# Latent attention scores as five fp32r products per pair of heads, each head on 64 rows

## The chip, the cores and the metric

The kernel runs on one core of one Trainium2 chip. A core has one TensorE (PE in the profile, its weight loads PEld), VectorE (DVE), ScalarE (ACT) and GpSimd (POOL), each working through its own instructions in the order in which the program lists them, and 16 DMA engines that are fed from queues, here those of SyncE (SP) and GpSimd. TensorE multiplies a stationary tile, loaded into the array beforehand, with a moving tile and adds into PSUM; the other engines read PSUM and SBUF. The metric is the device time of one execution in microseconds (us).

## The reference: what is computed

A decoder trunk of two layers over 512 tokens of width 1024, in float32. Layer 0 is a pooling and convolution mixer; layer 1 is multi-head latent attention, the part that changes. Each layer is followed by cross-attention into 256 memory tokens and a gated MLP.

```python
def mla_attention(h, cos, sin, ...):          # 16 heads, NOPE 64, ROPE 32, V_HEAD 64
    cq, ckv, k_pe = split(h @ w_dq_dkv, [384, 640])
    q = (rmsnorm(cq) @ w_uq).reshape(b, t, 16, 64 + 32)
    q_nope, q_pe = q[..., :64], apply_rope(q[..., 64:])
    kv = (rmsnorm(ckv) @ w_ukv).reshape(b, t, 16, 64 + 64)
    k_nope, v = kv[..., :64], kv[..., 64:]
    k_pe = apply_rope(k_pe)                   # one rotary key for all heads
    # per block i of 128 queries:
    s = (q_nope . k_nope + q_pe . k_pe) / sqrt(96)
    s = where(kpos <= qpos, s, -1e30)
    o = softmax(s) @ v
    return o @ w_o
```

Every score is thus a sum over 96 products: 64 of the content part, which has its own key per head, and 32 of the rotary part, whose key the heads share.

## The kernel before, in words

**Arithmetic.** Most products are made from fp32r operands. A float32 matrix is split into a high part (the value cast to fp32r) and a low part (the rest), and one product is three matmuls into the same PSUM bank: high by high, high by low, low by high (`mm3`, L177-181). A matrix is split in one of three ways: `load_w` (L168-175) fetches a weight by an SP DMA into `wr`, ACT casts it into `wh` (L173) and DVE subtracts into `wl` (L174), with both put early in the order (high priority); `low_by_dma` (L164-167) has ACT write minus the raw weight into `wl` and a GpSimd DMA add the raw weight to `wl`; `split_psum` (L207ff) has ACT cast a PSUM bank (L211) and DVE subtract (L212). The MLP's weights use the second way, with two buffers each of `wh1` and `wl1`.

**The stage.** `latent_attention` makes the low-rank queries `cq` (three 128-row tiles, high and low) and keys `ckv` (two tiles), then the one rotary key. After that come four groups of four heads. `group(g)` makes the four heads' rotary queries (`lin`, 9 matmuls of 512 columns) and turns them (`rotate`: a shuffle and three multiplications or sums on DVE); from the weights `ukv` and `uqn` it makes the content keys and queries (`contents`: `nope`, two banks of keys with 6 matmuls each, two of queries with 9 each). Two heads share a bank of 128 rows, 64 each. `group_values(g)` makes the values (`v`, 24 matmuls of 256 columns, two DVE copies).

**Scores before.** Each head has one operand of 128 rows for the query and one for the key: 64 rows of content, 32 of rotary part, 32 of zeros (kind A leaves the zeros off and uses 96). Four layouts, `qA`..`qD` and `kA`..`kD`, serve the four heads of a group. ACT copies the rotary rows (four copies of 32 rows, L1217, for a query) and one content half of each bank (64 rows, L1231), DVE the other half (L1232). `scores(n)` then makes four native float32 matmuls, one for each block of 128 queries against 128, 256, 384 and 512 keys (L1273, `s`; blocks 0 and 2 share a bank). DVE adds the mask and takes the row maximum of each block (L1275, called mask below), ACT makes the exponentials (L1281, four per head), DVE normalises (L1286).

**Around it.** `turn(n)` transposes the ten causal 128 by 128 blocks of a head's probabilities on PE (`t`, L1298) and ACT copies them out (L1300); `values(p)` multiplies those of two heads with `v` (L1310, `mpv`, two heads in the two halves of 64 columns). The loop over heads makes scores of head n, then, after every fourth head, the next group and its values, then `values` and `turn` of earlier heads (LAG = 2).

**What sets the order.** The program is written in this order and a scheduler places each engine's instructions by priority. At run time each engine keeps that order; an instruction that waits holds up all that stand behind it on its engine. PSUM has 8 banks, taken in turn.

Of the kernel before, what the change touches and what calls it, by code (L numbers as in the profile page):

```python
# [15 lines left out]
ALU = mybir.AluOpType  # L16
# [89 lines left out]
def kernel(ctx: ExitStack, tc: tile.TileContext, a):  # L106
# [988 lines left out]
    def rope_tables():  # L1095
# [41 lines left out]
    KIND = {  # L1137
        "A": (slice(0, 64), slice(64, 96), slice(96, 128)),
        "B": (slice(0, 64), slice(96, 128), slice(64, 96)),
        "C": (slice(64, 128), slice(0, 32), slice(32, 64)),  # L1140
        "D": (slice(64, 128), slice(32, 64), slice(0, 32)),
    }
    ORDER = ("A", "C", "B", "D")
    TILE = (("A", "C"), ("B", "D"))

    def latent_attention(norm, nxt, cs, sn, kv):
# [3 lines left out]
                           fill=NEG, base=0, channel_multiplier=1)  # L1150

# [17 lines left out]
        kacc, acc = slot("kacc"), slot("qacc")  # L1169
        kvp, cq, ckv = [], [], []  # L1170
# [29 lines left out]

        qb = {k: slot("q" + k) for k in KIND}
        kb = {k: slot("k" + k) for k in KIND}
        for k in KIND:
            for t in (qb[k], kb[k]):
                pool.memset(t[KIND[k][2], :], 0.0)

        def rotate(src, buf):
# [6 lines left out]
            vec.tensor_tensor(t, t, sw, ALU.add)  # L1214
            for k in KIND:
                rows = KIND[k][1]
                act.copy(buf[k][rows, :], t[rows, :])  # L1217
# [3 lines left out]
        rotate(kpe, kb)  # L1221

        def contents(buf, wh, wl, xs, nk):

            for i, (k0, k1) in enumerate(TILE):
# [4 lines left out]
                r0, r1 = KIND[k0][0], KIND[k1][0]  # L1230
                act.copy(buf[k0][r0, :], ps[r0, :])  # L1231
                vec.tensor_copy(buf[k1][r1, :], ps[r1, :])  # L1232
# [3 lines left out]
        kvw = {}  # L1236

        def group(g):

            rotate(linear(a["uqp"][g], cq), qb)  # L1240
            kvw[g] = wh, wl = load_w(a["ukv"][g], 1024)
            contents(kb, wh, wl, ckv, KKV)
            qh, ql = load_w(a["uqn"][g], 2 * KQ * P)
            contents(qb, qh, ql, cq, KQ)
# [18 lines left out]
        def scores(n):  # L1263
            kind = ORDER[n % 4]
            rows = slice(0, 96) if kind == "A" else slice(0, P)
            q, k = qb[kind][rows], kb[kind][rows]
            mx = small("mmx", [P, TB], bufs=3)
            banks = [bank("s") for _ in range(3)]
            ps = [banks[0][:, :P], banks[1][:, :2 * P], banks[0][:, P:], banks[2]]
            ts = [slot("p") for _ in range(3)]  # L1270
            ex = [ts[0][:, :P], ts[1][:, :2 * P], ts[0][:, P:], ts[2]]
            for i in (0, 2, 1, 3):
                pe.matmul(ps[i], q[:, i * P:(i + 1) * P], k[:, :P * (i + 1)], start=True, stop=True)  # L1273
            for i in (0, 2, 1, 3):
                vec.tensor_tensor_reduce(out=ex[i], in0=ps[i], in1=masks[:, T - P * (i + 1):], scale=1.0,  # L1275
                                         scalar=-3e38, op0=ALU.add, op1=ALU.max, accum_out=mx[:, i:i + 1])
# [36 lines left out]
        LAG = 2  # L1313
        proj = []
        group(0)
        for n in range(HEADS + LAG + 1):
            if n == HEADS:
                kv = fetch_kept(kv)
            if n < HEADS:
                scores(n)  # L1320
                if n == 0:
                    group_values(0)
                if n % 4 == 3 and n + 1 < HEADS:
                    group(n // 4 + 1)
# [126 lines left out]
```

## Time and profile before

| | |
|---|---|
| time, median of 3 runs | 1383.6 us (1383.36 to 1383.9) |
| the profiled execution | 1383.12 us, its span 1381.3 us |
| PE busy | 1352.6 us, 98% of the span |
| DVE busy | 1020.0 us, 74% |
| ACT busy | 748.8 us, 54% |
| the heads' part of latent attention, 738 to 868 us | 130 us |
| of it PE busy | 129.06 us |

The span is the time from the first to the last instruction that the profiler saw; the execution's own time is 1.8 us more. Busy time of PE counts matmuls whose ends are modelled, so a matmul of 512 columns shows 0.39 us though the next one starts 0.23 us later; spacings of starts are used below. In a timeline row the columns are the start and the length in us, the engine, the line, the operation, output and inputs, and how many instructions the row holds; a native float32 matmul shows as two instructions. Idle time before an instruction and what ended it stand in brackets.

### The profile page before, as it was taken

How to read it: one execution, taken by the hardware profiler on the slowest of the kernel's cores; microseconds unless marked ns; L12 is line 12 of the kernel's file. 1: busy time of each engine (PE TensorE's matmuls, PEld its weight loads, DVE VectorE, ACT ScalarE, POOL GpSimd, SP SyncE). 2: the span in 40 equal slices, each digit the busy share in tenths (PEclk: the TensorE clock that was granted, in tenths of full speed). 3: DMA queues.
4: the chain of work that ended last, by engine and by line, in shares of the span. 5: the costliest groups of instructions: out<-in, count | busy, mean ns of one | idle time of the engine just before them, and what ended most of it. 6: DMA issues, size and time to landing. Idle time of an engine off the chain costs nothing.

```text
span 1381.3 us, 20270 instructions
## 1 busy us (share of the span) xinstructions
PE 1352.6 (98%) x7756; PEld 1168.1 (85%) x7756; DVE 1020.0 (74%) x1897; ACT 748.8 (54%) x1264; POOL 52.9 (4%) x71
## 2 busy tenths in 40 slices
PE   8999999999989999999999999999999999999997
PEld 6888978888879999999887776888887899999987
DVE  6999989554787777776869775755549777777765
ACT  6416456445655555554447786644556555555433
POOL 0000000001100000000000000000011000000000
PEclk9999999999999999999999999999999999999999
DMA  9335634118835545553321113321486455555421
GB/s 327 99 104 188 217 104 151 61 38 207 184 91 130 159 124 138 134 137 94 106 81 50 43 47 107 107 77 61 124 188 124 130 132 143 134 136 144 111 73 62
DMA packets 57265, 168.01 MB, mean 122 GB/s; under 512 B 6480, under 2 KB 8144, under 8 KB 57168
## 3 DMA queue, kind: packets, MB, share of 16 engines
q1 hardware_dynamic: 47664, 135.55, 30.6%
q0 software_dynamic: 7776, 28.32, 12.3%
q10 hardware_dynamic: 1728, 2.86, 0.6%
q8 instruction: 60, 0.98, 0.3%
q14 instruction: 37, 0.30, 0.1%
HBM read 162.50 MB, written 4.19 MB: 121 GB/s over the span
## 4 chain that ended last, share of the span: by engine, by line
PE 88%; DVE 8%; ACT 2%; issue 1%; DMA 0%; SPq 0%; DVEq 0%; ACTq 0%
PE lin L179 11%; PE lin L181 11%; PE lin L180 11%; PE xyz L179 8%; PE xyz L180 8%; PE xyz L181 8%; PE down L180 4%; PE down L179 4%; PE down L181 4%; DVE cv L934 3%; PE s L1273 1%; PE mpv L1310 1%; DVE wl L174 1%; PE t L1298 1%; PE vx L180 1%
## 5 line engine op out<-in xcount | busy, mean ns | idle before, releaser
L179 PE MATMUL xyz<-th,wh 128*128 128x256 f32 x816 | 230.8, 284 | 10.6 <-ACT q L737 10.6
L181 PE MATMUL xyz<-th,wl 128*128 128x256 f32 x816 | 231.5, 284 | 0.0
L180 PE MATMUL xyz<-tl,wh 128*128 128x256 f32 x816 | 231.3, 284 | 0.0
L173 ACT CAST wh<-wr 128x1024 fp32r<-128x1024 f32 (+3 forms) x120 | 112.7, 944 | 161.8 <-issue 60.6
L179 PE MATMUL lin<-hh,wh 128*128 128x512 f32 x432 | 171.0, 396 | 5.9 <-ACT hh L286 5.9
L179 PEld LDWEIGHTS xyz<-th,wh 128*128 128x128 f32 x816 | 155.7, 192 | 23.2 <-ACT q L737 14.9
L180 PE MATMUL lin<-hl,wh 128*128 128x512 f32 x432 | 169.7, 393 | 0.0
L181 PE MATMUL lin<-hh,wl 128*128 128x512 f32 x432 | 169.2, 392 | 0.2 <-DVE wl L174 0.2
L180 PEld LDWEIGHTS xyz<-tl,wh 128*128 128x128 f32 x816 | 156.8, 192 | 7.1
L174 DVE TENSOR_TENSOR wl<-wr,wh 128x1024 fp32r<-128x1024 f32 (+3 forms) x120 | 130.1, 1086 | 42.4 <-ACT wh L173 40.9
L181 PEld LDWEIGHTS xyz<-th,wl 128*128 128x128 f32 x816 | 156.7, 192 | 0.0
L565 DVE TENSOR_TENSOR wl<-ws,wh 128x1024 fp32r<-128x1024 f32 x68 | 83.3, 1225 | 61.4 <-ACT wh L564 47.9
L564 ACT CAST wh<-ws 128x1024 fp32r<-128x1024 f32 x68 | 71.3, 1049 | 103.9 <-PE xyz L180 101.3
L179 PE MATMUL down<-fh,dwh 128*128 128x512 f32 x256 | 101.9, 398 | 1.2 <-ACT dwh L218 1.2
L180 PE MATMUL down<-fl,dwh 128*128 128x512 f32 x256 | 102.0, 398 | 0.0
L181 PE MATMUL down<-fh,dwl 128*128 128x512 f32 x256 | 100.5, 393 | 0.5 <-DVE dwl L219 0.5
L179 PEld LDWEIGHTS lin<-hh,wh 128*128 128x128 f32 x432 | 81.6, 189 | 22.3 <-ACT hh L286 6.2
L180 PEld LDWEIGHTS lin<-hl,wh 128*128 128x128 f32 x432 | 81.5, 189 | 18.5 <-DVE hl L287 2.7
L181 PEld LDWEIGHTS lin<-hh,wl 128*128 128x128 f32 x432 | 81.5, 189 | 17.5 <-DVE wl L174 0.6
L167 POOL DMA_DIRECT2D wl<-in_ffn_up x54 | 46.9, 868 | 1058.2 <-ACT wl L166 1058.2
L934 DVE SCALAR_TENSOR_TENSOR cv<-a,con,cv 128x509 f32<-128x509 f32 (+25 forms) x115 | 79.4, 726 | 0.1
L670 ACT ACTIVATE c<-c 128x512 f32<-128x512 f32 x44 | 27.8, 632 | 58.5 <-DVE c L669 58.3
(404 smaller groups left out, 3152.1 us busy)
## 6 DMA issues: line engine op xcount, KB each, us to landing
wr<-in_ffn_up SPq DMA_DIRECT2D x88, 512.0 KB, 4.1
wl<-in_ffn_up POOLq DMA_DIRECT2D x54, 512.0 KB, 5.7
dr<-in_ffn_down SPq DMA_DIRECT2D x64, 256.0 KB, 4.2
wr<-in_xa_wk SPq DMA_DIRECT2D x16, 512.0 KB, 3.5
wr<-in_xa_wv SPq DMA_DIRECT2D x16, 512.0 KB, 4.3
wr<-in_xa_wq SPq DMA_DIRECT2D x16, 512.0 KB, 3.5
wr<-in_xa_wo SPq DMA_DIRECT2D x16, 512.0 KB, 3.5
wr<-in_ffn_down SPq DMA_DIRECT2D x16, 384.0 KB, 3.3
```

The lines of the kernel that those rows point to most:

```text
L167: pool.dma_start(lo, src, accum_op=ALU.add)
L173: act.copy(hi[:, :n], raw[:, :n])
L174: vec.tensor_tensor(lo[:, :n], raw[:, :n], f(hi[:, :n]), ALU.subtract)
L179: pe.matmul(ps, ah, bh, start=first, stop=False, skip_group_check=more)
L180: pe.matmul(ps, ah, bl, start=False, stop=False, skip_group_check=more)
L181: pe.matmul(ps, al, bh, start=False, stop=last, skip_group_check=more)
L564: act.copy(hi[:, :n], raw)
L565: vec.tensor_tensor(lo[:, :n], raw, f(hi[:, :n]), ALU.subtract)
L670: act.activation(c, c, AF.Silu)
L934: vec.scalar_tensor_tensor(cv[i][:, s:], gl[i][:, :T - s], w, cv[i][:, s:], ALU.mult, ALU.add)
L1273: pe.matmul(ps[i], q[:, i * P:(i + 1) * P], k[:, :P * (i + 1)], start=True, stop=True)
L1298: pe.transpose(banks[b][:, c:c + P], prob[n][i][:, j * P:(j + 1) * P], ident)
```

## The change

1. Each pair of heads that shares a bank has its scores made together. The content queries and keys stay as high and low parts over 128 rows (`split_psum`, four per group in place of eight copies of 64 rows), head 0 in rows 0 to 63 and head 1 in rows 64 to 127. A block of scores is five fp32r matmuls for each head: high by high, high by low, low by high for the content, then two for the rotary part. The two heads' matmuls alternate and use rows 0 to 63 and 64 to 127 of the array.
2. For the rotary part, a head's 64 rows hold the query's high part in 32 rows and its low part in the other 32 (`rotary`: two ACT casts, four DVE subtractions of 32 rows). It is multiplied with `krh` (the key's high part in every 32 rows) and with `krl` (the key's low part under the query's high part, zeros elsewhere). The host puts the four heads' rotary columns in the order 0, 2, 1, 3.
3. The loop runs over pairs: blocks 0, 2, 1 of the pair, then `values` of the pair two back, `turn` of one earlier head, then block 3 and both softmaxes, then `turn` of the other head; after each second pair the next group with its values.
4. `ukv` and `uqn` no longer go through `load_w` but through `group_weights`: SP load, ACT cast into `wh1`, ACT negation into `wl1`, GpSimd DMA that adds. Group 0's weights are asked for at the start of the stage, group 1's after group 0's values, later ones two groups ahead.

The program has 256 matmuls more (scores 64 to 320), 8 DVE subtractions of weights fewer, 8 ACT negations and 8 GpSimd DMAs more.

```diff
+        def group_weights(g):
+            for src, n, out in ((a["ukv"][g], 1024, kvw), (a["uqn"][g], 2 * KQ * P, qw)):
+                raw = load_raw(src, n)
+                out[g] = hi, lo = early_parts()
+                act.copy(hi[:, :n], raw[:, :n])
+                low_by_dma(lo[:, :n], raw[:, :n], src)
...
         kacc, acc = slot("kacc"), slot("qacc")
+        group_weights(0)
...
-            for k in KIND:
-                rows = KIND[k][1]
-                act.copy(buf[k][rows, :], t[rows, :])
+            return t
...
-        rotate(kpe, kb)
+        t = rotate(kpe)
+        krh = slot("krh", F32R)
+        act.copy(krh, t)
+        krl = [slot("krl", F32R) for _ in range(2)]
+        for e in range(2):
+            pool.memset(f(krl[e]), 0.0)
+            for q in (e, e + 2):
+                r = slice(32 * q, 32 * q + 32)
+                vec.tensor_tensor(krl[e][r, :], t[r, :], f(krh[r, :]), ALU.subtract)
+
+        def rotary(src):
+            t = rotate(src)
+            out = []
+            for e in range(2):
+                q = slot("qr", F32R)
+                act.copy(q, t)
+                for h in range(2):
+                    r = slice(64 * h + 32 * e, 64 * h + 32 * e + 32)
+                    w = slice(64 * h + 32 * (1 - e), 64 * h + 32 * (1 - e) + 32)
+                    vec.tensor_tensor(q[w, :], t[r, :], f(q[r, :]), ALU.subtract)
+                out.append(q)
+            return out
...
-                r0, r1 = KIND[k0][0], KIND[k1][0]
-                act.copy(buf[k0][r0, :], ps[r0, :])
-                vec.tensor_copy(buf[k1][r1, :], ps[r1, :])
+                out.append(split_psum(ps, name))
+            return out
...
+            qr[g] = rotary(linear(a["uqp"][g], cq))
+            wh, wl = kvw[g]
+            kc[g] = contents(wh, wl, ckv, KKV, "kc")
+            qh, ql = qw.pop(g)
+            qc[g] = contents(qh, ql, cq, KQ, "qc")
...
-            for i in (0, 2, 1, 3):
-                pe.matmul(ps[i], q[:, i * P:(i + 1) * P], k[:, :P * (i + 1)], start=True, stop=True)
...
+        def scores(p, blocks):
+            g, e = p // 2, p % 2
+            for i in blocks:
+                s = slice(i * P, (i + 1) * P)
+                w = slice(0, (i + 1) * P)
+                passes = [(qc[g][e][x], kc[g][e][y]) for x, y in ((0, 0), (0, 1), (1, 0))]
+                passes += [(qr[g][e], krh), (qr[g][e], krl[e])]
+                for j, (q, k) in enumerate(passes):
+                    for h in range(2):
+                        r = ROWS[h]
+                        pe.matmul(open_heads[2 * p + h][1][i], q[r, s], k[r, w],
+                                  start=j == 0, stop=j == len(passes) - 1)
...
+        for p in range(pairs + 2):
+            if p < pairs:
+                open_pair(p)
+                scores(p, (0, 2, 1))
+            if p == 0:
+                group_values(0)
+                group_weights(1)
...
+            if 0 <= p - 2:
+                values(p - 2)
+            if 0 <= p - 1 < pairs:
+                turn(2 * p - 2)
+            if p < pairs:
+                scores(p, (3,))
+                softmax(2 * p)
+                softmax(2 * p + 1)
+            if 0 <= p - 1 < pairs:
+                turn(2 * p - 1)
+            if p % 2 == 1 and p + 1 < pairs:
+                group(p // 2 + 1)
+                group_values(p // 2 + 1)
+                if p // 2 + 2 < HEADS // 4:
+                    group_weights(p // 2 + 2)
```

The order of the instructions moves at three places that matter below. The first is **ACT at group 0**, after its content matmuls. Before, the copies that make `qA`..`qD` stand ahead of the next group's weight (`wh_7403`):

```order
L1231 COPY qA_7106<-nope_7190 64x512 [waits PE_49]
L1217 COPY qA_7106<-rot_7153 32x512 [waits DVE_49]
L1217 COPY qB_7107<-rot_7153 32x512
L1217 COPY qC_7108<-rot_7153 32x512
L1217 COPY qD_7109<-rot_7153 32x512
L1231 COPY qB_7107<-nope_7202 64x512 [waits PE_49]
L173 CAST wh_7403<-wr_7401 128x1024 [waits DMAHW7_49,Activation_49]
```

Now group 1's `ukv` (`wh_7300`, `wl_7301`), whose buffers are free once the last `nope` matmul of group 0 has read them, stands ahead of the rotary queries `qr` and of the content parts `kch`, `qch`:

```order
L1220 CAST krh_7128<-rot_7125 128x512 [waits DVE_49]
L1152 CAST wh_7300<-wr_7298 128x1024 [waits DMAHW6_49,PE_49]
L166 ACTIVATE wl_7301<-wr_7298 128x1024 [waits DMASW4_49,PE_49]
L1234 CAST qr_7160<-rot_7157 128x512 [waits DVE_49]
L1234 CAST qr_7164<-rot_7157 128x512
L211 CAST kch_7175<-nope_7168 128x512
L173 CAST wh_7881<-wr_7879 128x384 [waits DMAHW3_49,Activation_49]
L211 CAST kch_7186<-nope_7179 128x512
L211 CAST qch_7200<-nope_7190 128x512
```

The weight's two ACT instructions moved ahead of all that the first scores need. The second place is **ACT at group 1** (group 2 has the same order). Before:

```order
L1217 COPY qA_7106<-rot_7394 32x512 [waits DVE_49]
L1217 COPY qB_7107<-rot_7394 32x512
L1217 COPY qC_7108<-rot_7394 32x512
L1217 COPY qD_7109<-rot_7394 32x512
L1231 COPY qA_7106<-nope_7431 64x512 [waits PE_49]
L1231 COPY qB_7107<-nope_7443 64x512 [waits PE_49]
L173 CAST wh_7727<-wr_7725 128x1024 [waits DMAHW2_49,Activation_49]
```

And now, with the weights of group 2 (`wh_7588`, `wl_7589` from `ukv`; `wh_7595`, `wl_7596` from `uqn`):

```order
L1152 CAST wh_7588<-wr_7586 128x1024 [waits DMAHW1_49,PE_49]
L1234 CAST qr_7498<-rot_7495 128x512 [waits DVE_49]
L1234 CAST qr_7502<-rot_7495 128x512
L211 CAST kch_7513<-nope_7506 128x512
L166 ACTIVATE wl_7589<-wr_7586 128x1024 [waits DMASW6_49,PE_49]
L1152 CAST wh_7595<-wr_7593 128x768 [waits DMAHW2_49,PE_49]
L211 CAST kch_7524<-nope_7517 128x512
L166 ACTIVATE wl_7596<-wr_7593 128x768 [waits DMASW5_49]
L211 CAST qch_7538<-nope_7528 128x512
```

Four weight instructions moved in among the casts; `wh_7595` takes the buffer that the `v` matmuls of group 1 read. The third place is **PE at the first scores of group 1**. Now the scores of heads 4 and 5 (`s_7601`, `s_7608`) stand right behind the last `v` matmul:

```order
L181 MATMUL v_7571<-wh_7300,ckvl_7019 128x256
L1295 MATMUL s_7601<-kch_7513,qch_7538 128x128 [waits PE_49,Activation_49]
L1295 MATMUL s_7608<-kch_7513,qch_7538 128x128 [waits DVE_49]
L1295 MATMUL s_7601<-kcl_7514,qch_7538 128x128 [waits DVE_49]
L1295 MATMUL s_7608<-kcl_7514,qch_7538 128x128
L1295 MATMUL s_7601<-kch_7513,qcl_7539 128x128 [waits DVE_49]
...
L1295 MATMUL s_7609<-krl_7130,qr_7498 128x256
L1346 MATMUL mpv_7650<-pt_7403,v_7281 64x512
L1295 MATMUL s_7601<-kch_7513,qch_7538 128x384 [waits DVE_49]
L1295 MATMUL s_7608<-kch_7513,qch_7538 128x384 [waits DVE_49]
```

Before, a head's blocks 0 and 2 (128 and 384 keys), which share a bank, followed each other with no wait between them:

```order
L1273 MATMUL s_7565<-kC_7112,qC_7108 128x128 [waits PE_49]
L1273 MATMUL s_7565<-kC_7112,qC_7108 128x384
L1273 MATMUL s_7566<-kC_7112,qC_7108 128x256 [waits DVE_49]
L1273 MATMUL s_7567<-kC_7112,qC_7108 128x512 [waits DVE_49]
```

Now the 384-key block waits for DVE, which has to read block 0 first.

More of the change, by code (lines that the diff above doesn't have):

```diff
@@ L1135 @@
     SWAP = [(i + 16) % 32 for i in range(32)]
[L1137 to L1144, printed above, removed]
+    ROWS = (slice(0, 64), slice(64, 128))
     def latent_attention(norm, nxt, cs, sn, kv):
@@ L1199, in latent_attention, with rotate @@
         vec.tensor_scalar(rq, rq, SCALE, None, ALU.mult)
-        qb = {k: slot("q" + k) for k in KIND}
-        kb = {k: slot("k" + k) for k in KIND}
-        for k in KIND:
-            for t in (qb[k], kb[k]):
-                pool.memset(t[KIND[k][2], :], 0.0)
-        def rotate(src, buf):
+        def rotate(src):
             sw = slot("sw")
@@ L1214, in rotate, with contents @@
             vec.tensor_tensor(t, t, sw, ALU.add)
-            for k in KIND:
-                rows = KIND[k][1]
-                act.copy(buf[k][rows, :], t[rows, :])
+            return t
         kpe = slot("kpe")
         vec.tensor_tensor(kpe, kps, rb, ALU.mult)
-        rotate(kpe, kb)
-        def contents(buf, wh, wl, xs, nk):
-            for i, (k0, k1) in enumerate(TILE):
+        t = rotate(kpe)
[19 more added lines that the diff above has]
+            return out
+        def contents(wh, wl, xs, nk, name):
+            out = []
+            for i in range(2):
                 ps = bank("nope")
@@ L1261, in latent_attention @@
         o, prob, turned = [], {}, {}
[L1263 to L1271, printed above, removed]
-            for i in (0, 2, 1, 3):
[L1273 to L1276, printed above, removed]
+        open_heads = {}
@@ new lines, in scores @@
+        def scores(p, blocks):
[10 more added lines that the diff above has]
+                                  start=j == 0, stop=j == len(passes) - 1)
+                for h in range(2):
+                    mx, ps, ex = open_heads[2 * p + h]
+                    vec.tensor_tensor_reduce(out=ex[i], in0=ps[i], in1=masks[:, T - P * (i + 1):], scale=1.0,
+                                             scalar=-3e38, op0=ALU.add, op1=ALU.max, accum_out=mx[:, i:i + 1])
@@ new lines, in open_pair, with softmax @@
+        def open_pair(p):
+            for n in (2 * p, 2 * p + 1):
+                mx = small("mmx", [P, TB], bufs=4)
+                banks = [bank("s") for _ in range(3)]
+                ps = [banks[0][:, :P], banks[1][:, :2 * P], banks[0][:, P:], banks[2]]
+                ts = [slot("p") for _ in range(3)]
+                ex = [ts[0][:, :P], ts[1][:, :2 * P], ts[0][:, P:], ts[2]]
+                open_heads[n] = mx, ps, ex
+        def softmax(n):
+            mx, ps, ex = open_heads.pop(n)
@@ L1311, in values @@
             o.append(split_psum(ps, "mo"))
-        LAG = 2
         proj = []
         group(0)
-        for n in range(HEADS + LAG + 1):
-            if n == HEADS:
-                kv = fetch_kept(kv)
[L1319 to L1324, printed above, removed]
-                    group_values(n // 4 + 1)
-            if n >= HEADS - 1 and len(proj) < MLA_AHEAD:
+        pairs = HEADS // 2
+        for p in range(pairs + 2):
[5 more added lines that the diff above has]
+                group_weights(1)
+            if p == pairs:
+                kv = fetch_kept(kv)
+            if p >= pairs and len(proj) < MLA_AHEAD:
                 proj.append(Linear(a["mla_o"][len(proj)], KD))
                 proj[-1].run(o, 0, KD - 2)
-            ready = n - LAG - 1
-            if ready >= 0 and ready % 2 == 1:
-                values(ready // 2)
-            if 0 <= n - LAG < HEADS:
-                turn(n - LAG)
+            if 0 <= p - 2:
[13 more added lines that the diff above has]
+                    group_weights(p // 2 + 2)
         kv = split_kv(kv)
```

10 lines of the change are left out of this document (3 added, 7 removed).

## The prediction

> **What bounds the kernel now.** I read the page's shares and chain first, then the change's own stretch in windows, then that stretch on each engine. The page (core 0):
>
> ```profile
> span 1381.3 us, 20270 instructions
> PE 1352.6 (98%) x7756; PEld 1168.1 (85%) x7756; DVE 1020.0 (74%) x1897; ACT 748.8 (54%) x1264; POOL 52.9 (4%) x71
> PE 88%; DVE 8%; ACT 2%; issue 1%; DMA 0%; SPq 0%; DVEq 0%; ACTq 0%
> ```
>
> PE is busy 98% of the span and carries 88% of the chain that ends last. Windows over the heads' part, and over the three periods from one group's rotary projection (`lin`) to the next one's; the columns are the window, its length, busy time with instructions of PE, PEld, DVE, ACT and POOL, the granted clock, the DMA share and GB/s:
>
> ```profile
> 738.00:868.00 130.00, 129.06 (x697) 93.49 (x696) 90.91 (x291) 95.66 (x228) 0.00 (x0) 1.00 0.19 61
> 752.41:783.26 30.85, 30.61 (x169) 21.96 (x167) 23.38 (x75) 23.81 (x58) 0.00 (x0) 1.00 0.17 54
> 783.26:813.87 30.61, 30.61 (x169) 21.96 (x167) 22.77 (x71) 22.92 (x56) 0.00 (x0) 1.00 0.15 52
> 813.87:845.09 31.22, 30.97 (x169) 21.99 (x168) 23.82 (x73) 24.35 (x58) 0.00 (x0) 1.00 0.36 119
> ```
>
> Here PE waits for hardly anything; DVE and ACT are each busy for some 23.8 of 30.85 us. So PE time that is saved counts, and so does any wait that is put on PE. PE's timeline in the first period:
>
> ```profile
> 764.17 1.25 PE L1298 MATMUL t<-ident,p 128*128 128x128 f32 x10
> 765.26 2.32 PE L1273 MATMUL s<-kA,qA 96*128 96x128 f32 x8
> 767.51 2.37 PE L1310 MATMUL mpv<-pt,v 128*64 128x512 f32 x16
> 769.82 1.31 PE L1298 MATMUL t<-ident,p 128*128 128x128 f32 x10
> 770.97 2.32 PE L1273 MATMUL s<-kC,qC 128*128 128x128 f32 x8
> 773.13 1.04 PE L1298 MATMUL t<-ident,p 128*128 128x128 f32 x8
> ```
>
> By spacing of starts, ten transposes take 1.09 us (0.109 each), a head's scores 2.16 (770.97 to 773.13), two heads' `mpv` 2.22 of its 2.31. Scores before a tile of another shape (`mpv`) take 2.25, before `t` 2.16: a switch of shape costs 0.09.
>
> **Part 1, PE's own work.** A pair of heads costs 2 x 2.16 = 4.32 us now. The price of fp32r matmuls is seen where group 0's content ends, its first scores run and the next group begins:
>
> ```profile
> 738.23 0.39 PE L180 MATMUL nope<-cql,wh 128*128 128x512 f32 x1
> 738.46 0.39 PE L181 MATMUL nope<-cqh,wl 128*128 128x512 f32 x1
> 738.85 2.42 PE L1273 MATMUL s<-kA,qA 96*128 96x128 f32 x8
> 742.18 0.28 PE L179 MATMUL v<-wh,ckvh 128*128 128x256 f32 x1
> 742.30 0.28 PE L180 MATMUL v<-wl,ckvh 128*128 128x256 f32 x1
> 752.64 0.40 PE L180 MATMUL lin<-cql,wh 128*128 128x512 f32 x1
> ```
>
> 512 columns are spaced by 0.227, 256 by 0.12, and by that slope 384 take 0.173. No fp32r matmul of 128 columns is in this trace: the slope gives 0.067, the 256-column one bounds it at 0.12; I take 0.11, as the transposes of 128 columns. If the two heads of a pair run at the same time, each pass costs one matmul: 5 x (0.11 + 0.12 + 0.173 + 0.227) = 3.15. No row shows two halves of the rows at work; the nearest is `mpv`, two heads in the two column halves: 16 instructions over 5120 columns in 2.22 us against 2560 columns in 2.16 for `s`, so halves of columns overlap almost fully. I take 3.15, bounded by 6.3 (no overlap). Eight pairs save 8 x 1.17 = 9.4. In PE's order the shape changes 53 times where it was 22: 31 x 0.09 = +2.8. PE alone: **-6.6 us**.
>
> The Trainium skill, "TensorE: Matmul & The Clock Gate", Part 3 ("Measured speedup vs the span model"), gives 3.07 times for four row tiles rather than 4; the same loss on two would be, as an estimate from that page, 1.54, a pair of 4.1 us and a gain of 1.8 rather than 9.4. No run here shows it; it would put the sum up to 7.6 higher, 1411 if half of that falls into waits, and counts with the first rival below.
>
> **Part 2, the start of the heads.** In PE's order the first scores stand ahead of `v`, so all wait while their operands are made. ACT and DVE around that place:
>
> ```profile
> 738.18 0.61 ACT L1217 COPY qA<-rot 32x512 f32<-32x512 f32 x1 [0.54 <-DVE rot L1214]
> 741.33 1.05 ACT L173 CAST wh<-wr 128x1024 fp32r<-128x1024 f32 x1
> 742.39 1.28 ACT L1281 ACT_TABLE_LOAD   x1
> 763.17 0.58 ACT L1231 COPY qA<-nope 64x512 f32<-64x512 f32 x1
> ...
> 757.95 2.66 ACT p L1281 x8
> ...
> L173 ACT CAST wh<-wr 128x768 fp32r<-128x768 f32 x3 | 2.5, 835 | 0.0
> ...
> L166 ACT ACTIVATE wl<-wr x54: 1044/1057/1066, 316.5 to 1292.0; 128x1024 fp32r<-128x1024 f32 x54
> ...
> 739.17 0.69 DVE L1232 COPY qC<-nope 64x512 f32<-64x512 f32 x1
> 739.97 0.55 DVE L174 TENSOR_TENSOR wl<-wr,wh 128x384 fp32r<-128x384 f32 x1
> 740.63 0.29 DVE L1275 CUSTOM_DVE_ANT_0 p<-s,mask 128x128 f32<-128x128 f32 x1
> 748.50 1.27 DVE L1286 TENSOR_SCALAR p<-p,mrec 128x128 f32<-128x128 f32 x4
> ```
>
> Group 0's last `nope` ends near 738.7 in both kernels (start 738.46 plus one spacing). Now ACT has the weight cast of group 1 (1.05, waiting for that `nope`) and its negation (1.05) ahead: 740.8. Two `qr` casts at 0.62: 742.0; `kch`, a 384-column weight cast, `kch` of pair 1 and `qch` at 0.5 each: 744.0. DVE follows: four 32-row subtractions, each as long as a copy (0.6 spaced), until 743.8, then `kcl`, its pair-1 twin and `qcl` at 0.6: 745.6. PE went on to scores at once before (738.85); now it waits until 744.0 for `qch` and then until 745.6 for `qcl`. Block 2 then waits for the mask of block 0, which on DVE stands behind another low part (0.6) and a 384-column weight (0.55): 747.3. Blocks 2 and 1 (1.35) and `v` (24 x 0.12 = 2.88) end at 751.6. ACT has uqn's weight behind `v` (two of 0.83) and the table load (1.28): exponentials from 754.5, two heads at 2.66 to 759.8, norms of the second (0.15 + 1.27) 761.2, its last transposes 761.5. Then comes group 1's `lin`, before at 752.4 (one spacing ahead of 752.64); before, the second head's transposes (1.0) came only after it, so the comparable time is 753.4: **+8.1 us**, bounds 6 and 9 by 0.1 to 0.2 on each of a dozen steps.
>
> **Part 3, each later group.** PE in a period before: scores 8.63, `t` 4.36, `mpv` 4.42, `lin` and `nope` 39 x 0.227 = 8.85, `v` 2.88, switches 0.74: 29.9. After: minus 2 x 1.17, plus 0.7 for switches: 28.3. What is added is waits. From the start T of group 1's `lin`, `nope` ends at T + 8.9 and `v` at T + 11.7. ACT behind that `nope`: weight cast 1.05, two `qr` 1.2, `kch` 0.5, negation 1.05, weight cast 0.83 (whose buffer `v` frees), `kch` 0.5, negation 0.83, `qch` 0.5: T + 15.4; `qcl` on DVE a little behind it. PE waits 3.75 for `qch` and 0.45 for `qcl`. Block 2 waits for the mask of block 0 behind a weight, a `qcl` and two `v` copies: 1.05. In the middle of the group the transposes and the next pair's block 2 wait once for exponentials and norms (1.35) and once for a mask behind a reciprocal (1.2): these I read less surely. Sum 7.8, so 28.3 + 7.8 = 36.1 against 30.85: **+5.3** for group 1, and the same for group 2, whose order is the same. Group 3 has no weights behind it: boundary 3.6 (2.4 and 1.2), middle 2.55, 28.3 + 6.15 - 30.85 = **+3.6**.
>
> The engines have room in total: the eight 1024- and 768-column subtractions leave DVE, as many negations come to ACT, and the operands cost about +0.7 on each, so some 24.5 of 31 us; it is the order that makes PE wait. The eight accumulating DMAs on the GpSimd queue are issued after the negations and are needed a group later, over 25 us; at 5.7 us from issue to landing (the row of `wl<-in_ffn_up` below) they are covered, and would cost up to those 5.7 if not. SP's loads of group 0's weights move ahead of two others on its queue, which has 0% of the chain above: no cost.
>
> ```profile
> wl<-in_ffn_up POOLq DMA_DIRECT2D x54, 512.0 KB, 5.7
> 396.30:401.70 5.40, 0.01 (x1) 0.01 (x1) 5.39 (x10) 3.36 (x8) 0.00 (x0) 0.83 0.57 196
> 401.70:408.50 6.80, 6.80 (x31) 6.36 (x32) 3.23 (x6) 2.19 (x4) 0.00 (x0) 0.63 0.45 155
> 402.00:404.00 2.00, 2.00 (x11) 2.00 (x11) 2.00 (x4) 0.68 (x2) 0.00 (x0) 0.50 0.00 0
> ```
>
> **Part 4, the clock.** Elsewhere in this trace PE is idle for 5.4 us (396.3 to 401.7), and then the granted clock is 0.50, 0.63 over the 6.8 us behind it: 6.8 x 0.37 = 2.5 us lost. The start's wait (738.7 to 744.0) is as long. Part of the loss falls where PE waits anyhow: **+1.5**, bounds 0 and 2.5.
>
> **The sum.** 8.1 + 5.3 + 5.3 + 3.6 + 1.5 = 23.8 (the savings of Part 1 are inside the periods). The profiled execution took 1383.1, the median is 0.5 above it: 1383.1 + 23.8 = 1406.9, and 1407 is forecast.
>
> **The rivals.**
> *The halves do not run together.* Transposes of 128 columns, each with its own weight load, are 0.109 apart; if loads go one at a time, two heads' loads bind a pass at 0.22, and a pair is 5 x (3 x 0.22 + 0.227) = 4.4, 1.25 more than forecast, 10 for eight pairs; about half falls into waits: 1412. With nothing side by side, 25 more, 10 of it covered: 1422. For: no row shows row halves; against: `mpv`. Chance 0.12.
> *The clock drops at each boundary.* The 3.75 us waits would then cost up to 2.5 at three groups: 1407 + 7.5 = 1414. This trace has no idle time of that length to judge by. The Trainium skill, "TensorE: Matmul & The Clock Gate", Part 1 ("What's actually happening"), gives idle windows of about 3.4 us after which the clock is halved; the 5.4 us row agrees, and 3.75 us would be at its edge. Chance 0.08.
> *Only the start waits.* Group 1's `v` and the exponentials before it give ACT and DVE, which have 7 us of room in a period, the time to catch up; the later groups gain their 1.6: 1383.6 + 8.1 + 1.5 - 4.8 = 1388. Chance 0.09.
> *Faster.* The casts are all made under PE's other work, as the room would allow; only Part 1 is left: 1383.6 - 6.6 = 1377. For it the busy shares; against it the weights' place in ACT's order. Chance 0.11, and 0.04 for a cancellation near 1384.
> *The forecast*, 0.56.
>
> *Faster* is the other side of zero; it takes over from the point at which operands are ready when `v` ends. A change of 0.2%, 2.8 us, is about what a measurement of this kernel can tell from none: faster 0.11, within 0.04, slower 0.85. The forecast's own range is 1396 (half of Part 3's waits do not come: 10.9 less) to 1416. The range given runs from 1387, so that it holds the third rival, to 1420, short of the full loss of overlap; outside are the two cases of faster and of no change and about 0.04 above: 0.19.
>
> **What would show it.** At group 0, PE idle from 738.7 to 744 and to 745.6, with ACT's weight cast and negation ahead of `qr`. Periods between `lin` of groups 1, 2 and 3 of 36 us, with 4 us of idle PE behind `v`. A pair's blocks at 3.1 us where nothing waits; 4.4 or 6.3 there would show the first rival. A clock under 1.0 behind the start's wait. I am wrong if `lin` of group 1 starts under 757, or if the periods stay at 31 us.

## The result, and the profile after

The changed kernel takes 1428.16 us (median of 4 runs, 1427.12 to 1429.78) against 1383.65 of the kernel before: 1.0323 times as long, 95% interval 1.0305 to 1.0341, or 44.5 us more. 1407 had been forecast, from 1387 to 1420: the sign was right, the size half of what came.

The page of the profile after:

```profile
span 1425.9 us, 20659 instructions
PE 1376.8 (97%) x7948; PEld 1173.5 (82%) x7948; DVE 1027.6 (72%) x1909; ACT 746.1 (52%) x1261; POOL 56.5 (4%) x73
```

Windows of the kernel after, from the rotary projection (`lin`) of group 0 to that of group 1, of group 1 to 2, 2 to 3, and from group 3's to the first output projection; then the wait at the start and what follows it, the last part of that first period, and the wait at group 1 and what follows that (columns as in the prediction's windows):

```profile
734.72:771.47 36.75, 27.61 (x167) 22.20 (x165) 27.29 (x88) 15.89 (x33) 1.72 (x2) 0.81 0.27 56
771.47:810.94 39.47, 35.42 (x219) 25.39 (x217) 24.54 (x76) 24.57 (x59) 1.73 (x2) 0.91 0.27 69
810.94:850.84 39.90, 34.37 (x219) 24.85 (x217) 24.12 (x75) 24.03 (x58) 1.73 (x2) 0.91 0.25 63
850.84:889.09 38.25, 34.59 (x219) 25.37 (x217) 24.12 (x75) 20.66 (x54) 0.00 (x0) 0.91 0.21 69
743.90:749.88 5.98, 0.16 (x1) 0.00 (x1) 4.91 (x12) 5.01 (x9) 0.86 (x1) 0.70 0.46 77
749.88:756.50 6.62, 5.97 (x35) 5.26 (x36) 4.46 (x17) 0.43 (x1) 0.00 (x0) 0.50 0.48 118
764.30:771.47 7.17, 5.92 (x31) 4.11 (x31) 4.82 (x21) 4.47 (x14) 0.00 (x0) 0.76 0.17 33
783.65:786.60 2.95, 0.00 (x0) 0.00 (x0) 2.62 (x5) 2.95 (x6) 1.08 (x2) 1.00 0.49 85
786.60:793.50 6.90, 6.59 (x42) 4.15 (x43) 4.48 (x14) 1.95 (x3) 0.65 (x1) 0.75 0.95 232
```

The periods were 22.29 (729.71 to 752.00), 30.86, 30.61 and 31.21 us before. PE's timeline of the kernel before has the two starts:

```profile
729.71 0.48 PE L179 MATMUL lin<-cqh,wh 128*128 128x512 f32 x1
...
752.00 0.79 PE L179 MATMUL lin<-cqh,wh 128*128 128x512 f32 x1
```

Each of the later three is 7 to 9 us longer, and the granted clock, 1.00 throughout before, is 0.81 and 0.91 on average. It is 0.50 for 6.6 us behind the first wait, 0.76 over the 7.2 us ahead of group 1's `lin`, and 0.75 for 6.9 us behind the wait of group 1. By the trace's record of the granted clock, the stage has six stretches at 0.50, from 746.3, 766.8, 787.3, 804.4, 828.3 and 865.8, of 10.2, 3.4, 3.4, 3.4, 6.8 and 6.8 us: 34 us in all. What PE waited for in the stage (sum, number, longest):

```profile
PE s L1295 <- ACT qch L211: 12.4, 4, 5.8
PE s L1295 <- DVE mmx L1299: 3.7, 5, 1.1
PE s L1295 <- DVE qcl L212: 2.6, 4, 0.9
PE t L1334 <- DVE p L1322: 2.1, 4, 1.5
PE s L1295 <- DVE kcl L212: 1.2, 1, 1.2
```

The first scores wait at all four groups for `qch`, then for `qcl`, then block 2 for the mask (`mmx`). ACT's timeline at the start shows the order that the prediction read:

```profile
743.87 1.04 ACT L1152 CAST wh<-wr 128x1024 fp32r<-128x1024 f32 x1 [4.64 <-PE nope L180]
744.82 1.05 ACT L166 ACTIVATE wl<-wr 128x1024 fp32r<-128x1024 f32 x1
745.77 1.12 ACT L1234 CAST qr<-rot 128x512 fp32r<-128x512 f32 x2
...
748.35 0.51 ACT L173 CAST wh<-wr 128x384 fp32r<-128x384 f32 x1 [0.97 <-DMA wr<-in_uqp]
...
749.24 1.07 ACT L211 CAST qch<-nope 128x512 fp32r<-128x512 f32 x2
```

And PE's timeline: the first and the last `nope` of group 0, the first scores, and blocks of a later pair at full clock:

```profile
736.90 0.40 PE L179 MATMUL nope<-ckvh,wh 128*128 128x512 f32 x1
...
743.66 0.40 PE L181 MATMUL nope<-cqh,wl 128*128 128x512 f32 x1
749.88 0.47 PE L1295 MATMUL s<-kch,qch 64*128 64x128 f32 x2 [5.82 <-ACT qch L211]
...
795.63 0.50 PE L1295 MATMUL s<-kch,qch 64*128 64x512 f32 x2
795.97 0.39 PE L1295 MATMUL s<-kcl,qch 64*128 64x512 f32 x2
796.20 0.39 PE L1295 MATMUL s<-kch,qcl 64*128 64x512 f32 x2
...
796.99 1.31 PE L1334 MATMUL t<-ident,p 128*128 128x128 f32 x10
798.23 0.33 PE L1295 MATMUL s<-kch,qch 64*128 64x128 f32 x2
798.39 0.28 PE L1295 MATMUL s<-kcl,qch 64*128 64x128 f32 x2
798.51 0.28 PE L1295 MATMUL s<-kch,qcl 64*128 64x128 f32 x2
```

Two things stand there. A row of scores holds two matmuls, one of each head, and the next row starts 0.23 us later for 512 columns and 0.12 for 128 (and for 256, from 799.13 to 799.25): two heads cost the time of one. Only the first pass of a block is longer, 0.34 and 0.16, so that the block of 512 keys takes 1.36 up to the transposes. And the 30 `nope` matmuls, whose code did not change, are spaced by (743.66 - 736.90) / 29 = 0.233 us, where it was 0.227. That is outside every term of the prediction. Aligned by its matmuls, the program after is 5.0 us late when group 0's `lin` begins (734.72 against 729.71), before any changed matmul has run.

### The profile page after: what moved, and what is told of

Same layout as the page of the kernel before. It is cut to its first block, busy times and chain, and to the rows that moved or that the text cites. A ratio compares the mean times of both kernels' runs of the same rounds, so it can differ in the third digit from the quotient of the medians.

```text
span 1425.9 us, 20659 instructions
## 1 busy us (share of the span) xinstructions
PE 1376.8 (97%) x7948; PEld 1173.5 (82%) x7948; DVE 1027.6 (72%) x1909; ACT 746.1 (52%) x1261; POOL 56.5 (4%) x73
## 4 chain that ended last, share of the span: by engine, by line
PE 92%; DVE 3%; ACT 3%; issue 1%; DMA 0%; SPq 0%; DVEq 0%; ACTq 0%
PE lin L180 12%; PE lin L179 12%; PE lin L181 12%; PE xyz L179 8%; PE xyz L180 8%; PE xyz L181 8%; PE down L180 4%; PE down L181 4%; PE down L179 4%; PE s L1295 2%; PE kx L362 2%; ACT p L1317 1%; PE mpv L1346 1%; PE t L1334 1%; PE vx L181 1%; PE vx L179 1%
## 5 line engine op out<-in xcount | busy, mean ns | idle before, releaser
L181 PE MATMUL xyz<-th,wl 128*128 128x256 f32 x816 | 228.3, 280 | 0.0
L173 ACT CAST wh<-wr 128x1024 fp32r<-128x1024 f32 (+3 forms) x112 | 105.2, 943 | 173.3 <-issue 66.3
L174 DVE TENSOR_TENSOR wl<-wr,wh 128x1024 fp32r<-128x1024 f32 (+3 forms) x112 | 121.9, 1089 | 46.7 <-ACT wh L173 45.0
L166 ACT ACTIVATE wl<-wr 128x1024 fp32r<-128x1024 f32 (+1 forms) x62 | 64.6, 1042 | 8.6 <-PE v L180 8.6
```

The lines of the kernel that those rows point to most:

```text
L166: act.mul(lo, raw, -1.0)
L173: act.copy(hi[:, :n], raw[:, :n])
L174: vec.tensor_tensor(lo[:, :n], raw[:, :n], f(hi[:, :n]), ALU.subtract)
L181: pe.matmul(ps, al, bh, start=False, stop=last, skip_group_check=more)
```

## The experiments

Three theories were to be told apart: the **waits** themselves (and what makes them), the **clock** that falls behind them, and a third that the 0.233 suggested, **placement**. The change gives the small row-maximum tile `mmx` four buffers where it had three. In the program's memory layout each takes 32 bytes of every partition, and the slots of 2 KB in which nearly all operands lie come behind it, so all of them moved by 32 bytes, while the weight tiles `wh` and `wl` stayed.

### e1 and e5: placement alone, in either kernel

```diff
 # e1: the kernel before
-            mx = small("mmx", [P, TB], bufs=3)
+            mx = small("mmx", [P, TB], bufs=4)
 # e5: the kernel after
-                mx = small("mmx", [P, TB], bufs=4)
+                mx = small("mmx", [P, TB], bufs=3)
```

> The kernel before with one thing changed: the small row-maximum tile mmx has four buffers in place of three, as in the changed kernel, and every 2 KB slot allocated after it lies 32 bytes further on. Placement theory (in the changed kernel matmuls of 512 columns outside the change are spaced by 0.234 us where they were 0.227, and those of 256 columns by 0.117 where they were 0.120, because the slots moved by 32 bytes): 1388 to 1392, with 0.234 and 0.117 in its trace. Rival (the spacings are those of a run or a chip, or come from the new work): 1383 to 1385, 0.227 and 0.120.

> The changed kernel with three buffers of mmx, as before the change: every slot lies exactly where it lay before. Placement theory (a shift of 32 bytes cost the kernel before 6.6 us): 1420 to 1423, spacings of 0.227 and 0.120 outside the change. Rival (in the changed kernel the placement costs nothing, since the shift of 128 bytes gained nothing either; or three buffers add a wait): 1426 to 1431.

e1 takes 1390.0 us, 1.0049 (1.0034 to 1.0064) of the kernel before: 6.6 us for one more buffer of 32 bytes, which this kernel does not need. e5 takes 1421.63, 6.5 less than the kernel after, and 1.0280 (1.0264 to 1.0295) of the kernel before. The groups of matmuls by form in e1, whose code in them is that of the kernel before:

```profile
L180 PE MATMUL xyz<-tl,wh 128*128 128x256 f32 x816 | 228.8, 281 | 0.0
...
L180 PE MATMUL lin<-hl,wh 128*128 128x512 f32 x432 | 171.8, 398 | 0.0
```

In the kernel after the same two read 281 and 398 ns, in the kernel before (its page) 284 and 393, and in e5:

```profile
L180 PE MATMUL xyz<-tl,wh 128*128 128x256 f32 x816 | 231.0, 283 | 0.0
...
L180 PE MATMUL lin<-hl,wh 128*128 128x512 f32 x432 | 169.4, 392 | 0.0
```

With the buffer the matmuls of 512 columns become 5 ns longer and those of 256 columns 3 ns shorter; without it they go back. That it acts by the position of the slots, and not by what the heads do with `mmx`, is seen from where the time goes: 5.0 of the 6.6 us are lost before group 0's `lin` (734.69 in e1), ahead of any use of `mmx`, and e1's periods are within 0.2 us of those before (22.29, 30.95, 30.76, 31.38). Placement is shown, at 6.5 us of the 44.5.

### e2, e10, e11: other positions

```diff
 # e2: the kernel after, slots 128 bytes further on than in the kernel before
-                mx = small("mmx", [P, TB], bufs=4)
+                mx = small("mmx", [P, TB], bufs=7)
 # e10, e11: the kernel before, slots 64 and 96 bytes further on
-            mx = small("mmx", [P, TB], bufs=3)
+            mx = small("mmx", [P, TB], bufs=5)    # e11: bufs=6
```

> The changed kernel with seven buffers of mmx, so that the slots lie 128 bytes further on than before and have their old position within every 128 bytes. Placement theory: 1419 to 1423, spacings 0.227 and 0.120 again. Rival: 1427 to 1430 with 0.234 and 0.117 unchanged.

> The kernel before with five buffers of mmx: every slot 64 bytes further on. Placement theory (what counts is where a slot lies against the weight tiles, which stay): another pair of spacings for 512 and 256 columns, and a time that differs from 1383.4 by what they make, somewhere from 1377 to 1392. Rival (only multiples of 64 bytes matter, and 128 was as good as this one will be): 0.227 and 0.120, 1383 to 1385.

> The kernel before with six buffers of mmx: every slot 96 bytes further on. Placement theory: as e10, another pair of spacings, 1377 to 1392. Rival (odd multiples of 32 bytes are alike): the spacings of e1, 0.234 and 0.117, and its 1389 to 1391.

e2 takes 1432.73 us, 11.1 above e5 and above both of its ranges: a shift of 128 bytes is not no shift, and the expectation of e2 was wrong in this. e10 takes 1382.28, 0.9995 (0.9986 to 1.0005) of the kernel before and so the same; e11 takes 1397.66, 1.0109 (1.0094 to 1.0124), above both of its ranges. In e11 the two groups read 401 ns for 512 columns and 284 for 256.

Over four positions the kernel before spans 15 us, with no simple rule: 64 bytes are as good as none, 32 and 96 differ. What in the memory makes it was not tried. No position that was tried makes the kernel before faster.

### e4: the clock alone

```diff
                 open_pair(p)
+                if p % 2 == 0:
+                    for _ in range(25 if p == 0 else 12):
+                        pe.matmul(open_heads[2 * p][1][3], cq[0][0][:, :P], ckv[0][0], start=True, stop=True)
                 scores(p, (0, 2, 1))
```

> The changed kernel with 25 more matmuls of 512 columns ahead of group 0's first scores and 12 ahead of each later group's, into the PSUM bank of the pair's 512-key block, which the real scores then overwrite; their operands are long there, so they fill PE's wait for the casts and change nothing else. Clock theory (each wait halves the clock for some 7 us behind it, 13 us in all over the stage, where 1.5 was forecast): granted clock 1.00 behind the fillers and 1414 to 1420. Rival (the lost time is in the waits alone, or the clock falls because of the new matmuls themselves): 1427 to 1432.

e4 takes 1421.45 us, 6.7 below the kernel after, 1.0277 (1.0262 to 1.0293) of the kernel before, 1.5 above its range. Its later periods, and a piece behind its start:

```profile
771.80:808.85 37.05, 35.41 (x231) 25.85 (x229) 24.05 (x72) 24.61 (x59) 1.73 (x2) 1.00 0.29 74
808.85:846.18 37.33, 34.59 (x231) 25.72 (x229) 24.11 (x75) 24.04 (x58) 1.72 (x2) 1.00 0.27 68
846.18:882.57 36.39, 34.45 (x230) 25.60 (x229) 24.12 (x75) 20.67 (x54) 0.00 (x0) 1.00 0.23 73
...
750.30:754.00 3.70, 2.17 (x22) 1.83 (x24) 2.85 (x9) 0.61 (x2) 0.00 (x0) 1.00 0.39 71
754.00:757.00 3.00, 3.00 (x19) 2.77 (x17) 1.73 (x8) 0.00 (x0) 0.00 (x0) 0.53 0.51 172
```

With useless matmuls in the wait and nothing else changed, the clock of the three later periods is 1.00 and they are shorter by 2.4, 2.6 and 1.9: 6.9 us, all of e4's gain. The clock is shown to cost that at the later groups. At the start the fill gained nothing: the period from group 0's to group 1's `lin` is 36.52 us where it was 36.75. There the clock fell anyway, to 0.53 from 754 on, behind 3.7 us in which PE was busy for 2.17 with no wait over 1 us, and again for 3.4 us from 767.8. Of the 34 us at half clock e4 keeps these two stretches, 6.8 us.

### e3: the weights' path alone

```diff
-            wh, wl = kvw[g]
+            kvw[g] = wh, wl = load_w(a["ukv"][g], 1024)
             kc[g] = contents(wh, wl, ckv, KKV, "kc")
-            qh, ql = qw.pop(g)
+            qh, ql = load_w(a["uqn"][g], 2 * KQ * P)
 # and all calls of group_weights left out
```

> The changed kernel with the weights ukv and uqn made as before (load_w: ACT cast and DVE subtraction, early in the order; no negation, no GpSimd DMA, no group_weights). Waits theory (the weights' ACT instructions ahead of the first scores' casts make PE wait 5.8 us at the start and 3 at each later boundary, and each such wait is followed by a lowered clock): the first scores' wait for qch under 3 us, those of the later groups under 1.5, and 1408 to 1418. Rival (the casts and subtractions of the operands themselves are the wait): waits within 1 us of those of the changed kernel and 1424 to 1430.

e3 takes 1431.24 us, 3 more than the kernel after. PE still waits 10.7 us for `qch` (12.4 in the kernel after), and more for `kcl` and `qcl` (6.7 where it was 3.8). The waits theory missed: its first wait was to fall under 3 us and is 4.8. The rival missed its range by 1 us.

The edit does not clear the way of the operands, though. `load_w` still casts the weights on ACT, ahead of `qch` (1.04 us at 743.75; 1.05 at 782.56 and 0.83 at 785.63 in group 1), and its subtraction comes onto DVE, ahead of the subtractions for `qr` and `kcl` (1.23 us at 783.65). So e3 shows that the negations and the GpSimd DMAs are not the cause by themselves: DVE's subtractions in their place cost as much. How much of the wait is the weights' casts and how much the operands' own casts and subtractions was not separated.

### e6 and e7: work of PE between the operands and the scores

```diff
 # e6
-            if p < pairs:
-                open_pair(p)
-                scores(p, (0, 2, 1))
             if p == 0:
                 group_values(0)
                 group_weights(1)
+            if p < pairs and (p % 2 == 1 or p == 0):
+                open_pair(p)
+                scores(p, (0, 2, 1))
...
                 turn(2 * p - 2)
+            if p < pairs and p % 2 == 0 and p > 0:
+                open_pair(p)
+                scores(p, (0, 2, 1))
             if p < pairs:
                 scores(p, (3,))
 # e7: e6, mmx with bufs=3, and in scores() a second loop for the masks
+            for i in blocks:
                 for h in range(2):
                     mx, ps, ex = open_heads[2 * p + h]
```

> The changed kernel with other work of PE put between the content matmuls and the scores that need them: group 0's v ahead of its first scores, and at each later group the finished pair's mpv and the transposes of one head ahead of them. The casts, the weights and the scores themselves are as in the changed kernel. Cover theory (the operands' chain through ACT and DVE takes some 6 us behind the last nope, and only v, or nothing at group 0, covered it): the waits for qch and qcl fall from 15 us to under 5, the clock stays at 1.00 in the later periods, and 1402 to 1412. Rival (the waits move to the exponentials and transposes, which now come later): 1420 to 1430.

> The same order as in e6, with two more edits: three buffers of mmx, and the masks of blocks 0, 2, 1 after all three blocks' matmuls, so that block 2 need not wait for the mask of block 0. Cover theory: 6.6 below e6 by placement and 2 to 4 by the masks, 1393 to 1402. If what is then left is 1383 or less, PE's own saving of 6.6 us has come through. Rival (the masks, all at once, make the exponentials later): no more than 6.6 below e6.

e6 takes 1416.43 us, 11.7 below the kernel after; e7 takes 1401.65, 14.8 below e6 and 1.0133 (1.0118 to 1.0148) of the kernel before. e6 missed its range by 4 us, e7 met its own. Windows of e7's first two and last two periods, and what PE waits for in e7:

```profile
729.80:763.23 33.43, 26.35 (x166) 21.82 (x165) 27.35 (x89) 15.69 (x33) 1.72 (x2) 0.85 0.26 62
763.23:800.62 37.39, 31.85 (x219) 24.71 (x217) 24.25 (x72) 24.51 (x59) 1.72 (x2) 0.95 0.28 73
800.62:832.82 32.20, 30.18 (x219) 23.30 (x216) 23.84 (x75) 24.01 (x58) 1.72 (x2) 1.00 0.33 78
832.82:864.38 31.56, 29.79 (x219) 23.34 (x217) 23.85 (x75) 20.88 (x54) 0.00 (x0) 1.00 0.26 84
```

```profile
PE mpv L1347 <- ACT pt L1337: 4.8, 3, 1.7
PE s L1295 <- ACT pt L1337: 3.6, 1, 3.6
PE s L1295 <- ACT qch L211: 3.4, 1, 3.4
PE t L1335 <- DVE p L1323: 2.8, 1, 2.8
```

The wait for `qch` is left at the start alone, and the last two periods are within 1.6 us of the kernel before, at full clock. Two edits made this. The order alone (e6) has periods of 35.55, 39.64, 35.23 and 33.27: it took 4.7 and 5.0 us from the last two, with their clock, 1.2 from the start and nothing from group 1, where a wait of 3.8 us for a copy `pt` took the place of that for `qch`. The masks behind all blocks, with the old position of the slots, took another 2.1, 2.3, 3.0 and 1.7. So cover is what the first scores lacked at groups 2 and 3, and the block that waits for a mask was a loss of its own. What is left sits at the start (33.43 against 22.29) and in group 1 (37.39 against 30.86).

### e9 and e12: the two waits that are left in e7

```diff
 # e9: e7 and the edit of e3
 # e12: e7, and the loop that makes krl moved behind group 0's rotary queries
         group(0)
+        key_low()
```

> The kernel of e7 with the weights made as before the change (load_w, as in e3). In e7 group 1's period still has PE waiting 3.6 us for a copy on ACT that stands behind the cast of an output weight, whose load came late because its buffer was held until the negation. Theory (with the operands covered, the weights' path is the next wait): group 1's period from 37.4 to 33 or 34, the first wait for qch from 3.4 to under 2, 1393 to 1398. Rival (e3 again: DVE's subtractions, early in the order, delay the operands as much as the negations did): 1400 to 1405.

> The kernel of e7 with the four subtractions that make the rotary key's low part krl put behind group 0's rotary queries in the program. On DVE group 0's rotation then ends some 2.7 us earlier, and on ACT the casts of qr and of the first kch stand ahead of group 1's weight casts, as they did before the change. Order theory of the start (the weights' casts stand ahead only because the rotation is late): the first wait for qch falls from 3.4 to under 1.5 and group 0's period from 33.4 to 30 or 31, 1397 to 1400. Rival (DVE's own work, 12 subtractions of 0.6 to 0.7 us ahead of the first complete block, sets the time, whatever stands ahead on ACT; krl is now last): a wait for krl of 2 us or more takes the place of that for qch, and 1400 to 1403.

e9 takes 1403.53 us, no better than e7. Group 1's period does fall, to 32.9 us, but the others rise and the start stays at 34.6: the waits move (`mpv` for ACT's copies `pt` 7.9 us where it was 4.8). e12 takes 1399.36, 1.0121 (1.0104 to 1.0138) of the kernel before, 2.3 below e7. Two of PE's waits in it:

```profile
PE t L1338 <- DVE p L1326: 3.4, 1, 3.4
...
PE s L1298 <- DVE krl L1229: 0.5, 1, 0.5
```

The wait for `qch` is gone, as the order theory had it, and 0.5 us for `krl` came in its place. But group 0's period only fell to 32.1, not to 30 or 31, and the transposes' wait for the probabilities grew from 2.8 to 3.4. In all the changed forms both heads' exponentials stand behind all their blocks, which would make such a wait; no run tested that by itself. e12 is the best of the changed forms that were run, and none beats the kernel before.

### e8: the two heads not in turn

```diff
-                for j, (q, k) in enumerate(passes):
-                    for h in range(2):
+                for h in range(2):
+                    for j, (q, k) in enumerate(passes):
                         r = ROWS[h]
```

> The changed kernel with the five passes of one head and then the five of the other, in place of the two heads in turn. Side-by-side theory (two halves of the rows work at the same time only where they stand next to each other in PE's order): a pair's passes of 512 columns are spaced by 0.227 each, a pair costs 6.3 us where it cost 3.15, and with half of the 25 us in PE's waits the time is 1436 to 1446. Rival (PE runs both in any order, or not at the same time even now): 1426 to 1431.

e8 takes 1436.33 us, 1.0385 (1.0370 to 1.0401) of the kernel before: the time lies at the lower edge of what the side-by-side theory expected, and yet its mechanism is not what happened. PE's timeline of one 512-key block, whose order in the program is all five of the first head, then all five of the second:

```profile
792.22 0.49 PE L1295 MATMUL s<-kch,qch 64*128 64x512 f32 x1
792.55 0.39 PE L1295 MATMUL s<-kcl,qch 64*128 64x512 f32 x1
792.56 0.50 PE L1295 MATMUL s<-kch,qch 64*128 64x512 f32 x1
792.78 0.39 PE L1295 MATMUL s<-kch,qcl 64*128 64x512 f32 x1
```

The second head's first pass starts at 792.56, ahead of the first head's third at 792.78: the two halves of the rows run beside each other, 0.34 us apart, though the program lists them one after the other. PE did not keep the program's order between the two halves, so what is said ahead of the prediction, that each engine keeps that order at run time, does not hold for them. A block costs 1.71 us (792.22 to the transposes at 793.93) where it cost 1.36 in turn (795.63 to 796.99 in the kernel after), not 2.3. The clock of the three later periods is 0.92, 0.88 and 0.84 where it was 0.91 in each; how the 8.2 us divide between blocks, waits and clock was not worked out.

## Why the prediction was right in sign and wrong in size

What failed above all is Part 4: the clock was given 1.5 us, once, and took some 10. Placement, 6.5 us, was in no part. In the other parts the waits were found in the right places, and their sizes were off.

**Part 1, PE's own work: right in its mechanism, too cheap in its price.** The passes measured 0.12, 0.12 and 0.23 for 128, 256 and 512 columns (0.11, 0.12 and 0.227 forecast), and the overlap of the halves, taken from the column halves of `mpv`, is real. The first rival, no overlap, is refuted, and e8 shows that the program's order costs a block 0.35 us and not the overlap. By the Trainium skill, "TensorE: Matmul & The Clock Gate", Part 3, four row tiles gave 3.07 times; that loss carried over to two would make a pair 4.1 us, an estimate from that page. The trace shows no such loss in a pass (0.23 us for two heads, 0.233 for one `nope`). But a whole pair takes 3.5 us, not 3.15: blocks of 1.36 (795.63), 1.35 (128 and 256 keys, 798.23 to 799.58) and 1.08 (384 keys, 791.01 to 792.09), less three switches of 0.09. The first pass of each block is what was left out. Where the heads are out of step, as for one pair of e7 (848.37 to 852.36, less one switch), it takes 3.9. Eight pairs then save 3 to 6.5 us, not 9.4.

**Part 2, the start: the place and the wait right, the way to group 1's `lin` too short.** The wait for `qch` was forecast at 5.3 us and came as 5.8; another 0.58 for `qcl`. The period is 36.75 against 22.29, 13.5 after taking off the 1.0 for the second head's transposes, where 8.1 and a share of 1.5 were forecast. With 5.0 us taken off for the late start of the stage, the chain can be laid beside the forecast. The 384-key block starts 0.6 us late (747.9 for 747.3), with a load that ACT's 384-column cast waited for (0.97 in the row above) ahead of it. `v` ends 2.3 late (753.9 for 751.6): from the 384-key block on these matmuls ran at 0.50 (the row up to 756.5), which took 1.7, near the 1.5 of Part 4. The probabilities are ready 2.35 late, so nothing more went wrong on the way. But the last transposes, forecast for 761.5, end at 766.5. In PE's order the 512-key block of the next pair stands ahead of them; the forecast left it out, and it ran at half clock:

```profile
768.07 0.79 PE L1295 MATMUL s<-kch,qch 64*128 64x512 f32 x1
...
770.40 1.31 PE L1334 MATMUL t<-ident,p 128*128 128x128 f32 x10
```

That is 2.6 us more. The stretch at 0.50 from 766.8 to 770.2, in which PE was busy throughout, can have cost half of its 3.4 us, so 1.7 as an estimate; 0.9 is then left for the block. The last 0.4 us is a misreading: group 1's `lin` began at 752.00 in the kernel before (its row stands above), not at 752.4. e12 shows that the order of the start can be mended at the operands and is then held at the exponentials, so no single instruction was the price of it.

**Part 3, the later groups: nearly right in number, by errors that partly cancel.** At full clock (e4) the periods are 6.2, 6.7 and 5.2 us above those before, where 5.3, 5.3 and 3.6 were forecast. The sum took 28.3 and the waits for the period after and set the measured 30.85 against them, while the same sum gives 29.9 for the period before: that put each of the three some 0.9 too low. The waits came shorter, 4.1, 5.5 and 3.5 us in all for 7.8, 7.8 and 6.15: in group 1, PE stood 2.97 us for `qch` and 0.29 for `qcl` (3.75 and 0.45 forecast), and 0.2 and 0.6 in the middle of it (1.35 and 1.2). PE's own time came longer, by 0.7 to 1.5 for two pairs at the prices of Part 1 and by a rest that was not split further. The new spacing of `lin` and `nope` is little of it: with the old one (e5) these periods are 39.27, 39.82 and 38.31.

The prediction blamed the weights that stand in front of the casts. The time at which `qch` came was right (15.4 us behind `lin` forecast, 15.15 measured: 786.62 from 771.47), but e3 did not part the weights from the operands' own work, so this stays open. What e6 shows is that the wait hurts because nothing of PE's work but `v` lies between the last content matmul and the scores; in the kernel before, a head's ten transposes lay there (764.17 in the prediction's rows), and the first scores needed the operands of one head only.

**Part 4, the clock: wrong, the mis-sized term.** It was given 1.5 us, once, at the start, and the recurrence at each boundary was a rival with a chance of 0.08 and a price of 7.5. That rival was right: e4 measures 6.9 us for the three later periods, and the start has a second fall, 1.7 by the estimate of Part 2, beside the first. The step that failed is "This trace has no idle time of that length to judge by", out of which a low chance was made. Waits of 2.97 and 0.29 us were enough: behind them the clock was 0.75 for 6.9 us. By the Trainium skill's same page, Part 1, the clock is halved after an idle window of about 3.4 us. The measurement differs and decides: the waits at the later groups stayed under that, and in e4 a stretch with PE busy for 2.17 of 3.70 us was followed by half clock.

**What no part held: placement.** The sum let all of the program outside the stage keep its time. A buffer count in the change, three to four, took that away, by 6.5 us (e5) or 6.6 (e1).

The terms as measured: start 13.5, later groups at full clock 18.1 (6.2 + 6.7 + 5.2), clock at these 6.9, placement 6.5. That is 45.0 against 44.5, with 0.5 us counted twice: so much shorter are the four periods of e5 with the old spacing. Of the 21 us that the forecast lacked, the clock has 8.8 (6.9, the 1.7 of the second fall and 0.2 of the first), placement 6.5, the later groups at full clock 3.9, and the rest of the start 1.9.

## What to carry to other kernels

When a product is made of more, shorter operands, the operands' casts and subtractions become a chain of their own: put other work of the bounding engine between the matmuls that feed them and those that use them. What is left uncovered can cost twice, once as a wait and once as a lowered clock behind it. Fillers in such a wait show its clock part by themselves. Hold the addresses of all else fixed when a change is measured, or measure the shift alone; here one buffer of 32 bytes made a seventh of the result.

## What the runs showed of the hardware

- The position of operands in SBUF sets the pace of matmuls, by up to 2% here: shifts of 32, 64 and 96 bytes of the slots, with the weights in place, gave 1390.0, 1382.3 and 1397.7 us for the kernel before (1382.8 to 1383.4 beside them), and mean lengths of 398, 393 and 401 ns for one group of 512-column matmuls.
- Matmuls on the two halves of the rows overlap fully in a pass (0.23 us for a pair of 512 columns; the first pass of a block 0.34), and overlap even when the program lists all of one half first: one of the second half then started at 792.56, ahead of one of the first half, listed earlier, at 792.78 (e8).
- The clock fell to a half behind interrupted idleness: 1.5 us of 3.7, in pieces under 1 us (e4). Each stretch at half clock in the stage lasted 3.4 us or two or three times that (3.4, 6.8 and 10.2 in the kernel after).
- A DVE subtraction of 32 rows by 512 columns takes as long as one of 128 rows. In the kernel after, the groups of the low parts of `qr` and of `qcl` read:

```profile
L1238 DVE TENSOR_TENSOR qr<-rot,qr 32x512 fp32r<-32x512 f32 x16 | 10.9, 682 | 5.1 <-ACT qr L1234 4.9
...
L212 DVE TENSOR_TENSOR qcl<-nope,qch 128x512 fp32r<-128x512 f32 x8 | 5.2, 684 | 0.3 <-ACT qch L211 0.3
```
